# Retention in a two-layer trunk: rotation tables times R made once, one sum on GpSimd behind the swap, rotated tiles by turns of the pairs, y passes and stores later

## The chip, the cores and the metric

The kernel runs on one core of a Trainium2 chip. The core has five engines with an instruction queue each: TensorE (PE in the profile; PEld is its weight loads), VectorE (DVE), ScalarE (ACT), GpSimd (POOL) and SyncE (SP). SyncE here does little but issue DMA transfers, in order. An engine works through its queue in order, so an instruction that waits holds up all that stand behind it. The metric is the time of the program on the device in microseconds (us), median of several runs.

## The reference

A trunk of two layers on x of 1024 frames by 1024 channels, in float32. Layer 0 projects the normalised input to six parts and feeds two branches; the part that the change touches is retention, with rotary positions on q and k:

```python
def rope(x, positions):
    ...
    x1, x2 = x[..., :half], x[..., half:]
    return jnp.concatenate([x1 * cos - x2 * sin, x1 * sin + x2 * cos], axis=-1)

def retention(q, k, v):
    q = rope(q.astype(f32), positions) * (RET_DK ** -0.5)
    k = rope(k.astype(f32), positions)
    ...
    scores = jnp.einsum('bnihd,bnjhd->bnhij', qc, kc) * intra
    intra_out = jnp.einsum('bnhij,bnjhe->bnihe', scores, vc)
    kv = jnp.einsum('bnjhd,jh,bnjhe->bnhde', kc, k_dec, vc)
    ...
    _, s_prev = lax.scan(state_step, zeros, kv)
    cross = jnp.einsum('bnihd,ih,bnhde->bnihe', qc, q_dec, s_prev)
    out = normalised per head of (intra_out + cross)

def s5_mixer(u, ...):
    y = scan over chunks of a diagonal complex state space
    y = jax.nn.gelu(y)
    y = y * jax.nn.sigmoid(y @ glu_w + glu_b)
```

There are 8 heads of 64 (k, q) and 128 (v) channels, and 16 chunks of 64 frames. Each branch is multiplied by its SiLU gate, both go through one output projection, and layer 1 is a convolution module. R below is the reciprocal root mean square of each frame in layer 0: the projections run on x as it is, and their results are multiplied by R.

## The kernel before

**Arithmetic.** A float32 product is made of three matmuls with tiles split into a high and a low part (`mm3`: high by high, high by low, low by high). So every weight load `wf_…` is followed by a cast `wh_…` on ScalarE (L252) and a subtraction `wl_…` on GpSimd or VectorE (L253), and a projection of 128 channels by 512 frames (a half) is 24 matmuls into one PSUM bank, `mm_…`. The projections use a pool of 3 banks, most other products a pool of 5.

**Stages of layer 0.** The S5 scan and the gate projections fill the first 308 us. Then come the value products (`mm_v`, L1360) with sums of parts of x (`xt1` to `xt4`, a Strassen-like scheme), then four pairs of heads. A pair is projected (k, then q) while TensorE works through the heads of the pair before. The GLU of the S5 branch (`mm_glu`) begins before pair 3 ends, with a scheme of the same kind: it needs sums of weights (`gs`, written to DRAM as `ws_d`) and of y (`yn`, written as `yn_d` and, as differences, `t_d`).

**A pair (`ret_proj`, `ret_heads`).** VectorE writes `kraw` or `qraw` = bank times R, a half at a time (L1242). Rotation needs each 32-row block's partner, so four DMAs on SyncE write `kswp`/`qswp`, the tile with its blocks swapped (L1251, 128 KB each). GpSimd multiplies raw by the cosine table (L1255, into `krot`/`qrot`) and the swapped tile by the sine table (L1257), and VectorE adds them (L1258): 4 GpSimd and 2 VectorE instructions a tensor. The tables, `ropek`, are 1 MB, loaded at the start of the stage. Then TensorE transposes krot (`ktp`, L1372), VectorE scales it (`kt`, L1374), and TensorE makes `kv` (L1391), from which VectorE steps the state `S` (L1399, L1401), and the scores `sp` from qrot and krot (L1408); VectorE masks them (`sc`, L1414), and TensorE makes the output `ro` (L1435, L1440). It is normalised on VectorE and ScalarE (`bn`, `rs`, `off`, `on`; L1449 to L1457), transposed (`rt`), multiplied by the gate (`grl`, L1468) and stored (`yr_d`, L1471).

**The y passes (`y_pass`, L1125 to L1160).** The S5 output lies in DRAM in 8 blocks. Pass k (0 to 3) takes blocks k and k+4: load (`yp`, L1134), gelu on ScalarE (L1144), store of `yn_d` (L1146), four 128x512 subtractions on VectorE (L1150 to L1153), and for each of the two a high part `th` on ScalarE (L1157), its store (L1158), a low part on VectorE (L1159) and its store (L1160). Passes 0 and 1 run among the value products, a step at a time; passes 2 and 3 behind pairs 0 and 1, all through one buffer, tag `yp`: the load of block k+4 waits for the gelu of block k, and the second high part for the store of the first.

**What sets the order.** The program is written in one sequence, and a scheduler sorts it into the queue of each engine. `issue_after` holds instructions behind another, and the table `ORDER` names pairs on an engine: in (engine, late, early) the instruction of the one tile comes behind that of the other. Tiles with the same tag share `bufs` buffers, so that a new one waits for the readers of the old. `self.late` collects stores that `flush` issues some stages later, on SyncE.

Of the kernel before, what the change touches and what calls it, by code (L numbers as in the profile page):

```python
# [11 lines left out]
F32 = mybir.dt.float32  # L12
# [3 lines left out]
ALU = mybir.AluOpType  # L16
# [3 lines left out]
P = 128  # L20
# [18 lines left out]

LANES = 2  # L40
ORDER = (
    ('PE', ('turn', 0), ('mm_u6_0', 23)),
# [7 lines left out]
    ('DVE', ('cv6_0', 23), ('h1l0_1', 0)),  # L50
    ('SP', ('yt2h0', 0), ('qswp_3', 3)),
    ('PE', ('mm_oc2_1_0', 2), ('mm_oc0_1_0', 6)),
    ('DVE', ('mm_gluy3', 1), ('mm_gluz0', 0)),
# [74 lines left out]
class Trunk:  # L128
# [995 lines left out]
    def y_pass(self, k, yp=None, tag="ynt"):  # L1124
# [24 lines left out]
        (b11, b12), (b21, b22) = ((y[:, :HALF], y[:, HALF:]) for y in yns)  # L1149
        v.tensor_tensor(b22, b22, b12, op=ALU.subtract)  # L1150
        v.tensor_tensor(b12, b12, b11, op=ALU.subtract)
        v.tensor_tensor(b11, b22, b11, op=ALU.add)
        v.tensor_tensor(b21, b11, b21, op=ALU.subtract)  # L1153
        yield
# [8 lines left out]
    def glu_sums(self, g):  # L1163
# [13 lines left out]
        for i in range(2):  # L1177
            nc.sync.dma_start(self.ws_d[i, m, :, :, c].rearrange("p j k n -> p j (k n)"), q[i])

    def retention(self, st):  # L1180
# [5 lines left out]
        self.rk = rq.tile([P, 2, T], F32, name="ropek")  # L1186
        nc.sync.dma_start(self.rk[:], A["rope_k"])
        self.g128 = rp.tile([P, 4], F32, name="g128")
        nc.sync.dma_start(self.g128[:], A["ret_g128"])
# [8 lines left out]
        V = self.ret_values(vw)  # L1198
        for n, steps in enumerate(((0,), (0,), (1,), (1,), (1,), ())):
            next(V)  # L1200
            with self.tc.issue_after(self.last_evac.ins) if n == 3 else nullcontext():
                for i in steps:
                    next(y[i])
# [24 lines left out]
    def ret_proj(self, pair):  # L1228
        nc, A, rp = self.nc, self.A, self.rp
        mask = rp.tile([P, 2, P], F32, name=f"retmask_{pair}", tag="retmask", bufs=2)  # L1230
        nc.sync.dma_start(mask[:], A["ret_mask"][:, 2 * pair:2 * pair + 2])
        kdec = self.kdec[:, 2 * pair:2 * pair + 2]
        raws, tabs = {}, {"k": self.rk, "q": self.rk}

        def project(nm):
            w = self.wnext(f"{nm}{pair}")
            raw = raws[nm] = self.rq.tile([P, T], F32, name=f"{nm}raw_{pair}", tag="raw", bufs=2)
            for h in range(2):
                c = slice(h * HALF, (h + 1) * HALF)
                ps = self.bank(f"mm_{nm}{pair}_{h}", aux=False)  # L1240
                self.gemm(ps[:], w, self.xs[h])
                self.last_raw = nc.vector.tensor_tensor(nat(raw[:, c]), un(ps[:]), nat(self.R[:, c]), op=ALU.mult)  # L1242
            return self.last_raw

        def turn(nm, behind=None):
            raw, tab = raws[nm], tabs[nm]
            swp = self.rq.tile([P, T], F32, name=f"{nm}swp_{pair}", tag="swp", bufs=2)
            o = rp.tile([P, T], F32, name=f"{nm}rot_{pair}", tag=f"{nm}rot", bufs=1)
            for b in range(4):
                s = b ^ 1  # L1250
                self.last_swap = nc.sync.dma_start(swp[32 * b:32 * b + 32, :], raw[32 * s:32 * s + 32, :])  # L1251
            cs = [slice(h * HALF, (h + 1) * HALF) for h in range(2)]

            for c in cs:
                nc.gpsimd.tensor_tensor(o[:, c], raw[:, c], tab[:, 0, c], op=ALU.mult)  # L1255
            for c in cs:
                self.last_turn = nc.gpsimd.tensor_tensor(swp[:, c], swp[:, c], tab[:, 1, c], op=ALU.mult)  # L1257
            return o, [lambda c=c: nc.vector.tensor_tensor(o[:, c], o[:, c], swp[:, c], op=ALU.add) for c in cs]  # L1258


        project("k")
        yield None
        krot, adds = turn("k")
        last = project("q")
        with self.tc.issue_after(last.ins):
            for add in adds:
                add()
        qrot, qadds = turn("q")
        if pair % 2 == 0:
            for add in qadds:  # L1270
                add()
            qadds = ()
        yield krot, qrot, qadds, mask, kdec

    def ret_values(self, vw):
# [8 lines left out]
        def sums(name, k0, h):  # L1284
            res = []
            for i in range(2):
                f = self.rq.tile([P, 2, HALF], F32, name=f"{name}f{i}", tag="raw", bufs=2)
                nc.sync.dma_start(f[:], self.tx_d[k0 + 2 * i:k0 + 2 * i + 2, :, cs(h)].rearrange("k p t -> p k t"))
                for k in range(2):
                    a, b = (self.op_tile(vw, "t", f"{name}{q}{2 * i + k}") for q in "hl")  # L1290
                    nc.scalar.copy(a[:], f[:, k])
                    nc.gpsimd.tensor_tensor(b[:], f[:, k], a[:].bitcast(F32), op=ALU.subtract)
                    res.append((a, b))
# [769 lines left out]
def _shape_constants():  # L2063
# [5 lines left out]
    cos, sin = np.cos(ang), np.sin(ang)  # L2069
    rope = np.stack([np.concatenate([cos, cos] * 2, 0), np.concatenate([-sin, sin] * 2, 0)], 1)  # L2070
    c["rope_k"] = rope.astype(f)
# [73 lines left out]
```

## Time and profile before

| | |
|---|---|
| median of 3 runs | 1147.41 us (1146.99 to 1149.24) |
| profiled execution, and its span | 1148.62 us, 1146.5 us |
| granted TensorE clock, mean | 0.991 |
| value products | about 333 to 411 us |
| four pairs of heads | about 411 to 562 us |
| GLU of the S5 branch | about 532 to 633 us |

The page gives the busy time of each engine and its costliest groups. In a row of a timeline the first two numbers are start and length in us, then the engine, the line, the operation, out<-in, the number of instructions, and in brackets the idle time ahead and what ended it. Only an idle TensorE costs time directly: it is the engine that is nearly always busy.

### The profile page before, as it was taken

How to read it: one execution, taken by the hardware profiler on the slowest of the kernel's cores; microseconds unless marked ns; L12 is line 12 of the kernel's file. 1: busy time of each engine (PE TensorE's matmuls, PEld its weight loads, DVE VectorE, ACT ScalarE, POOL GpSimd, SP SyncE). 2: the span in 40 equal slices, each digit the busy share in tenths (PEclk: the TensorE clock that was granted, in tenths of full speed). 3: DMA queues.
4: the chain of work that ended last, by engine and by line, in shares of the span. 5: the costliest groups of instructions: out<-in, count | busy, mean ns of one | idle time of the engine just before them, and what ended most of it. 6: DMA issues, size and time to landing. Idle time of an engine off the chain costs nothing.

```text
span 1146.5 us, 16992 instructions
## 1 busy us (share of the span) xinstructions
PE 1109.6 (97%) x6014; PEld 965.9 (84%) x6014; DVE 831.2 (73%) x1444; ACT 543.8 (47%) x835; POOL 662.9 (58%) x463
## 2 busy tenths in 40 slices
PE   9999999999997998898899999999999999999997
PEld 8888888888885887777788888888888888888886
DVE  7877767777426564869558731499999989999744
ACT  7323334443224724425536523555544667446773
POOL 3059957878425425756377011389643468788863
PEclk9999999999998999999999999999999999999999
DMA  8445667776988656696998998566678665356964
GB/s 314 118 138 162 205 222 250 245 260 247 322 239 280 222 200 202 225 344 227 373 381 309 331 335 283 192 239 203 223 256 296 236 210 192 120 176 229 332 239 172
DMA packets 136117, 279.48 MB, mean 244 GB/s; under 512 B 21088, under 2 KB 50016, under 8 KB 135904
## 3 DMA queue, kind: packets, MB, share of 16 engines
q1 hardware_dynamic: 129744, 257.16, 66.8%
q10 hardware_dynamic: 6288, 21.24, 4.7%
q8 instruction: 47, 0.77, 0.3%
q14 instruction: 38, 0.31, 0.1%
HBM read 191.65 MB, written 82.51 MB: 239 GB/s over the span
## 4 chain that ended last, share of the span: by engine, by line
PE 76%; DMA 10%; DVE 5%; ACT 4%; issue 2%; POOL 2%; SPq 1%; POOLq 0%; ACTq 0%; DVEq 0%
PE mm_g L274 6%; PE mm_g L275 6%; PE mm_g L276 6%; PE mm_wo L274 5%; PE mm_wo L275 5%; PE mm_wo L276 5%; PE mm_v L1360 3%; PE mm_b L275 2%; PE mm_b L276 2%; PE mm_a L276 2%; PE mm_a L275 2%; PE mm_a L274 2%; PE mm_b L274 2%; PE mm_u L276 2%; PE mm_u L275 2%
## 5 line engine op out<-in xcount | busy, mean ns | idle before, releaser
L1762 DVE SCALAR_TENSOR_TENSOR cv<-u,convw,cv 128x512 f32<-128x512 f32 x390 | 267.7, 748 | 6.0 <-ACT cv L1729 3.9
L1723 POOL TENSOR_TENSOR tp<-tp,tp 128x512 f32<-128x512 f32 x64 | 82.4, 1288 | 33.1 <-ACT tp L1722 32.2
L274 PE MATMUL mm_g<-xh,wh_g 128*128 128x512 f32 x256 | 97.7, 382 | 0.0
L275 PE MATMUL mm_g<-xl,wh_g 128*128 128x512 f32 x256 | 97.0, 379 | 0.0
L276 PE MATMUL mm_g<-xh,wl_g 128*128 128x512 f32 x256 | 95.9, 379 | 0.0
L541 POOL TENSOR_TENSOR s1q<-s1q,s1q 128x512 f32<-128x512 f32 x12 | 16.7, 1391 | 81.0 <-ACT s1q L536 81.0
L1722 ACT ACTIVATE tp<-u,convw 128x512 f32<-128x512 f32 x64 | 45.3, 718 | 32.1 <-POOL tp L1723 31.3
L276 PEld LDWEIGHTS mm_g<-xh,wl_g 128*128 128x128 f32 x256 | 48.4, 189 | 6.9
L274 PEld LDWEIGHTS mm_g<-xh,wh_g 128*128 128x128 f32 x256 | 48.4, 189 | 6.9 <-issue 0.2
L275 PEld LDWEIGHTS mm_g<-xl,wh_g 128*128 128x128 f32 x256 | 48.4, 189 | 6.6
L275 PE MATMUL mm_oc<-zl,wh_woc 128*128 128x512 f32 (+1 forms) x144 | 51.4, 357 | 0.2 <-DVE zl L1477 0.2
L274 PE MATMUL mm_oc<-zh,wh_woc 128*128 128x512 f32 (+1 forms) x144 | 51.0, 363 | 0.0
L276 PE MATMUL mm_oc<-zh,wl_woc 128*128 128x512 f32 (+1 forms) x144 | 50.8, 356 | 0.0
L253 POOL TENSOR_TENSOR wl_glu<-wf_glu,wh_glu 128x1024 fp32r<-128x1024 f32 x14 | 33.8, 2422 | 27.1 <-DMA wf_glu<-ws_d 12.3
L274 PE MATMUL mm_wo<-ysh,wh_wos 128*128 128x512 f32 x128 | 48.9, 382 | 0.0
L274 PE MATMUL mm_g<-h1h,wh_cg 128*128 128x512 f32 x128 | 48.9, 382 | 0.0
L275 PE MATMUL mm_wo<-ysl,wh_wos 128*128 128x512 f32 x128 | 48.5, 379 | 0.0
L274 PE MATMUL mm_a<-h1h,wh_ca 128*128 128x512 f32 x128 | 48.5, 379 | 0.0
L276 PE MATMUL mm_wo<-ysh,wl_wos 128*128 128x512 f32 x128 | 48.5, 379 | 0.0
L276 PE MATMUL mm_b<-h1h,wl_cb 128*128 128x512 f32 x128 | 48.5, 379 | 0.0
L276 PE MATMUL mm_g<-h1h,wl_cg 128*128 128x512 f32 x128 | 48.5, 379 | 0.0
L275 PE MATMUL mm_a<-h1l,wh_ca 128*128 128x512 f32 x128 | 48.5, 379 | 0.0
(647 smaller groups left out, 3550.8 us busy)
## 6 DMA issues: line engine op xcount, KB each, us to landing
wf_g<-w_ab SPq DMA_DIRECT2D x16, 512.0 KB
wf_wos<-w_out SPq DMA_DIRECT2D x16, 512.0 KB
wf_wor<-w_out SPq DMA_DIRECT2D x16, 512.0 KB
wf_cb<-w_c SPq DMA_DIRECT2D x16, 512.0 KB
wf_ca<-w_c SPq DMA_DIRECT2D x16, 512.0 KB
wf_woc<-w_out_c SPq DMA_DIRECT2D x16, 512.0 KB
wf_cg<-w_c SPq DMA_DIRECT2D x11, 512.0 KB
x<-xT SPq DMA_DIRECT2D x8, 512.0 KB
```

Source lines behind the costliest of these rows:

```text
L253: self.low_made = lo[i].tensor_tensor(wl[:].rearrange(fl)[:, c], wf[:, c], h.bitcast(F32), op=ALU.subtract)
L274: nc.tensor.matmul(ps, wh[:, kb, :], xh, start=start, stop=False, **more)
L275: nc.tensor.matmul(ps, wh[:, kb, :], xl, start=False, stop=False, **more)
L276: self.last_mm = nc.tensor.matmul(ps, wl[:, kb, :], xh, start=False, stop=stop, **more)
L541: nc.gpsimd.tensor_tensor(a, a, sq[:], op=ALU.add)
L1360: nc.tensor.matmul(us[b][:], l[:, o], r, start=fresh and k == n == 0, stop=k == 3 and n == 2, **({} if fresh else {"skip_group_check": True}))
L1722: nc.scalar.mul(sk[:], u[:, k:k + HALF], cw[:, nb, k:k + 1])
L1723: gp.tensor_tensor(s0[:], s0[:], sk[:], op=ALU.add)
L1762: v.scalar_tensor_tensor(dst[:], *tap, accs_[i][:], op0=ALU.mult, op1=ALU.add)
```

## The change

- The tables are multiplied by R once: four 128x512 multiplications on GpSimd behind the load (L1217 of the changed kernel). From a bank VectorE then writes two products, raw (bank times the sine table) and the rotated tile (bank times the cosine table), L1275. The swap moves the product, so the signs of the sine table are turned round in the host's constants, and one addition a half on GpSimd (L1282) ends the rotation.
- raw and swapped tiles have one buffer each instead of two. krot and qrot of even pairs lie in one pool and those of odd pairs in another; the loads `xt…f` take the buffers of the odd ones instead of those of raw.
- Steps of y passes 0 and 1 stand two to four turns of the value products later. The four subtractions of passes 2 and 3 run on GpSimd. Stores of `ws_d` go to `self.late`.
- ORDER gains 23 rows. They put stores (`ws_d`, `yr_d`) and loads (`gs`, `grl`) of SyncE behind the swaps of pairs 1 to 3, the subtractions of passes 2 and 3 behind the q sums of pairs 1 and 2, casts of y behind others of ScalarE, and output products of pair 2 behind the q projection of pair 3.

```diff
+ADDS = {"k": lambda nc: nc.gpsimd, "q": lambda nc: nc.gpsimd}
 ORDER = (
...
+    ('SP', ('grl_6', 0), ('qswp_3', 3)),
+    ('Pool', ('yn_6', 0), ('qrot_1', 1)),
...
+    ('SP', ('ws_d', 6), ('qswp_3', 3)),
...
+    ('PE', ('ro0_4', 0), ('mm_q3_1', 23)),
+    ('Activation', ('th0_3', 0), ('on_5_1', 3)),
...
@@ y_pass
-        v.tensor_tensor(b22, b22, b12, op=ALU.subtract)
...
+        eng = nc.gpsimd if held else v
+        eng.tensor_tensor(b22, b22, b12, op=ALU.subtract)
...
@@ glu_sums
         for i in range(2):
-            nc.sync.dma_start(self.ws_d[i, m, :, :, c].rearrange("p j k n -> p j (k n)"), q[i])
+            self.late.append((1, lambda i=i: nc.sync.dma_start(self.ws_d[i, m, :, :, c].rearrange("p j k n -> p j (k n)"), q[i])))
@@ retention
         nc.sync.dma_start(self.rk[:], A["rope_k"])
+        for n in (1, 0):
+            for c in (slice(0, HALF), slice(HALF, T)):
+                nc.gpsimd.tensor_tensor(self.rk[:, n, c], self.rk[:, n, c], self.R[:, c], op=ALU.mult)
...
-        for n, steps in enumerate(((0,), (0,), (1,), (1,), (1,), ())):
+        for n, steps in enumerate(((), (), (0,), (0, 1), (1,), (1,))):
@@ ret_proj
+            raw = self.rq.tile([P, T], F32, name=f"{nm}raw_{pair}", tag="raw", bufs=1)
+            swp = self.rq.tile([P, T], F32, name=f"{nm}swp_{pair}", tag="swp", bufs=1)
+            o = (rp if pair % 2 else self.rq).tile([P, T], F32, name=f"{nm}rot_{pair}", tag=f"{nm}rot{pair % 2}", bufs=1)
...
-                self.last_raw = nc.vector.tensor_tensor(nat(raw[:, c]), un(ps[:]), nat(self.R[:, c]), op=ALU.mult)
+                for n, dst in ((1, raw), (0, o)):
+                    last = nc.vector.tensor_tensor(nat(dst[:, c]), un(ps[:]), nat(self.rk[:, n, c]), op=ALU.mult)
...
-                nc.gpsimd.tensor_tensor(o[:, c], raw[:, c], tab[:, 0, c], op=ALU.mult)
-            for c in cs:
-                self.last_turn = nc.gpsimd.tensor_tensor(swp[:, c], swp[:, c], tab[:, 1, c], op=ALU.mult)
-            return o, [lambda c=c: nc.vector.tensor_tensor(o[:, c], o[:, c], swp[:, c], op=ALU.add) for c in cs]
+                self.last_turn = eng(nc).tensor_tensor(o[:, c], o[:, c], swp[:, c], op=ALU.add)
@@ ret_values
-                f = self.rq.tile([P, 2, HALF], F32, name=f"{name}f{i}", tag="raw", bufs=2)
+                f = self.rp.tile([P, 2, HALF], F32, name=f"{name}f{i}", tag=f"{'kq'[i]}rot1", bufs=1)
```

How the queues change is shown at three places. The number behind a name's last underscore is the instance of a tile; "x2" is two like instructions. On VectorE, between the q projection of pair 1 and its first state step, there stood before:

```order
L1242 TENSOR_TENSOR qraw_1_4316<-mm_q1_1_4343,R0_356 128x512
L1258 TENSOR_TENSOR krot_1_4301<-krot_1_4301,kswp_1_4300 128x512 x2
L1150 TENSOR_TENSOR yn_6_4410<-yn_6_4410,yn_2_4404 128x512
L1151 TENSOR_TENSOR yn_2_4404<-yn_2_4404 128x512
L1152 TENSOR_TENSOR yn_2_4404<-yn_6_4410,yn_2_4404 128x512
L1242 TENSOR_TENSOR kraw_2_4643<-mm_k2_0_4644,R0_356 128x512
L1153 TENSOR_TENSOR yn_6_4410<-yn_2_4404,yn_6_4410 128x512
L1374 TENSOR_TENSOR kt_1_4426<-ktp0_1_4427,kdec_3344 128x512
L1374 TENSOR_TENSOR kt_1_4426<-ktp1_1_4433,kdec_3344 128x512
L1159 TENSOR_TENSOR yn_2_4404<-yn_2_4404,th0_2_4418 128x1024
L1258 TENSOR_TENSOR qrot_1_4372<-qrot_1_4372,qswp_1_4371 128x512 x2
L1242 TENSOR_TENSOR kraw_2_4643<-mm_k2_1_4670,R0_356 128x512
```

and now stands:

```order
L1275 TENSOR_TENSOR qraw_1_4316<-mm_q1_1_4346,ropek_3340 128x512
L1275 TENSOR_TENSOR qrot_1_4318<-mm_q1_1_4346,ropek_3340 128x512
L1388 TENSOR_TENSOR kt_1_4420<-ktp0_1_4421,kdec_3348 128x512
L1388 TENSOR_TENSOR kt_1_4420<-ktp1_1_4427,kdec_3348 128x512
L1275 TENSOR_TENSOR kraw_2_4639<-mm_k2_0_4642,ropek_3340 128x512
L1275 TENSOR_TENSOR krot_2_4641<-mm_k2_0_4642,ropek_3340 128x512
L1413 COPY S_1_4433<-kv0_1_4434 128x128
L1415 SCALAR_TENSOR_TENSOR S_1_4433<-S_1_4433,g128_3346,kv0_1_4434 128x128 x3
```

The four subtractions of y pass 2 (L1150 to L1153) and the additions of the rotation (L1258) are gone from here, the low part of y (L1159) stands further back, and each bank has two evacuations.

On GpSimd, at the same place of the program, there stood (behind the cosine products of q):

```order
L253 TENSOR_TENSOR wl_vm_4639<-wf_vm_4637,wh_vm_4638 128x1024
L1257 TENSOR_TENSOR qswp_1_4371<-qswp_1_4371,ropek_3340 128x512 x2
L1173 TENSOR_TENSOR gs1_0_4382<-gs1_0_4382 128x512
L1174 TENSOR_TENSOR gs1_0_4382<-gs0_0_4381,gs1_0_4382 128x512
L1175 TENSOR_TENSOR gs0_0_4381<-gs1_0_4382,gs0_0_4381 128x512
```

and now:

```order
L279 TENSOR_TENSOR wl_vm_4631<-wf_vm_4629,wh_vm_4630 128x1024
L1282 TENSOR_TENSOR qrot_1_4318<-qrot_1_4318,qswp_1_4317 128x512 x2
L1200 TENSOR_TENSOR gs1_0_4380<-gs1_0_4380 128x512
L1177 TENSOR_TENSOR yn_6_4404<-yn_6_4404,yn_2_4398 128x512
L1201 TENSOR_TENSOR gs1_0_4380<-gs0_0_4379,gs1_0_4380 128x512
L1178 TENSOR_TENSOR yn_2_4398<-yn_2_4398 128x512
L1202 TENSOR_TENSOR gs0_0_4379<-gs1_0_4380,gs0_0_4379 128x512
L1179 TENSOR_TENSOR yn_2_4398<-yn_6_4404,yn_2_4398 128x512
L1203 TENSOR_TENSOR gs0_0_4379<-gs0_0_4379 128x512
L1180 TENSOR_TENSOR yn_6_4404<-yn_2_4398,yn_6_4404 128x512
```

The k sum of pair 1 now stands ahead of the weights wl_vm; the subtractions of y pass 2 stand among the sums of GLU weights, by turns.

On TensorE, where pair 3 begins (`mm_glu11` is a product of the GLU, `rt` the transposes of the heads of pair 2), there stood:

```order
L274 MATMUL mm_glu11_5526<-y11h3_5491,wh_glu0_5104 128x512
L1372 MATMUL ktp0_3_5246<-ident_69,krot_3_5163 128x128 x4
L1372 MATMUL ktp1_3_5252<-ident_69,krot_3_5163 128x128 x4
L275 MATMUL mm_glu11_5526<-y11l3_5492,wh_glu0_5104 128x512
L276 MATMUL mm_glu11_5526<-y11h3_5491,wl_glu0_5105 128x512
L1391 MATMUL kv0_3_5265<-v_00_3507,kt_3_5245 64x128 x8
L1391 MATMUL kv1_3_5278<-v_01_3508,kt_3_5245 64x128 x6
L1408 MATMUL sp00_3_5290<-qrot_3_5236,krot_3_5163 128x128
L1408 MATMUL sp01_3_5291<-qrot_3_5236,krot_3_5163 128x128
```

and now:

```order
L302 MATMUL mm_glu11_5514<-y11h3_5479,wl_glu0_5093 128x512
L1479 MATMUL rt0_5_5063<-ident_69,on_5_0_5000 128x128 x4
L1479 MATMUL rt0_4_5069<-ident_69,on_4_0_4980 128x128 x4
L1479 MATMUL rt1_5_5075<-ident_69,on_5_1_5058 128x128 x4
L1479 MATMUL rt1_4_5081<-ident_69,on_4_1_5038 128x128 x4
L1386 MATMUL ktp0_3_5236<-ident_69,krot_3_5103 128x128 x4
L1386 MATMUL ktp1_3_5242<-ident_69,krot_3_5103 128x128 x4
L1405 MATMUL kv0_3_5253<-v_00_3507,kt_3_5235 64x128 x8
L1405 MATMUL kv1_3_5266<-v_01_3508,kt_3_5235 64x128 x6
L1422 MATMUL sp00_3_5278<-qrot_3_5174,krot_3_5103 128x128
L1422 MATMUL sp01_3_5279<-qrot_3_5174,krot_3_5103 128x128
```

The GLU products between ktp, kv and sp of pair 3 now stand ahead of them, and so do the transposes of pair 2. Before, 12 more GLU products stood between the first row of sp10_3 and the first of sp11_3; they no longer do.

64 lines of the change are left out of this document (35 added, 29 removed).

## The prediction

> **What bounds the kernel now.** I read the page first, for the engine that carries the span, then the waits of that engine, then its busy time by stage.
>
> ```profile
> span 1146.5 us, 16992 instructions
> PE 1109.6 (97%) x6014; PEld 965.9 (84%) x6014; DVE 831.2 (73%) x1444; ACT 543.8 (47%) x835; POOL 662.9 (58%) x463
> ```
>
> TensorE is busy for 1109.6 of 1146.5 us, so at most 36.9 us of the span can be had by taking its waits away, plus whatever a higher clock gives. The profiled execution took 1148.62 us, 2.1 more than its span, and lies 1.2 above the median of the runs, 1147.41. All terms below are taken from 1148.62, and 1.2 is subtracted at the end. The waits of TensorE between 308 and 562 us (engine, line, the one waited for; total, times, longest) say where the idle time is:
>
> ```profile
> PE kv L1391 <- DVE kt L1374: 5.9, 3, 4.4
> PE sp L1408 <- DVE qrot L1258: 5.9, 3, 5.1
> PE mm_v L1360 <- ACT v L1310: 5.7, 2, 2.9
> PE sp L1408 <- DVE S L1401: 2.9, 2, 1.6
> PE mm_v L1360 <- DVE wl_vc L253: 1.8, 1, 1.8
> PE ktp L1372 <- DVE krot L1258: 1.8, 2, 1.1
> PE mm_v L1360 <- DVE wl_vj L253: 1.7, 1, 1.7
> ```
>
> These seven rows add to 25.7 us: 70% of all TensorE idle time stands in this stretch, which is also where the change works. No row is long; each is an in-order engine that had something else in front. The windows (us, busy time and count of PE, PEld, DVE, ACT, POOL; granted clock, DMA share, GB/s) split it by stage:
>
> ```profile
> 344.00:410.00 66.00, 56.64 (x242) 47.85 (x243) 38.78 (x35) 35.62 (x50) 32.06 (x21) 0.92 0.80 269
> ...
> 449.00:472.00 23.00, 15.86 (x115) 13.15 (x114) 17.47 (x22) 4.32 (x4) 16.08 (x8) 0.93 0.77 256
> ...
> 530.00:562.00 32.00, 25.37 (x190) 21.39 (x189) 25.58 (x51) 8.84 (x20) 11.60 (x8) 0.95 0.88 301
> 562.00:626.00 64.00, 62.99 (x298) 54.45 (x297) 42.47 (x72) 37.46 (x61) 45.66 (x27) 1.00 0.97 353
> ```
>
> TensorE idles 9.4 us in the value products, 7.1 in pair 1, 6.6 in pair 3, and in the GLU stage behind them 1.0, where the DMA engines are 0.97 busy: there is no room for more bytes there. No engine is full in the stages with waits, so they are latency and order, not throughput.
>
> **The change part by part.** Durations first, from the tile views (shortest, median, longest ns of one):
>
> ```profile
> L1242 DVE TENSOR_TENSOR kraw<-mm_k,R x8: 668/684/693, 317.3 to 525.9; 128x512 f32<-128x512 f32 x8
> L1255 POOL TENSOR_TENSOR krot<-kraw,ropek x8: 1269/1278/2264, 325.7 to 526.7; 128x512 f32<-128x512 f32 x8
> L1257 POOL TENSOR_TENSOR qswp<-qswp,ropek x8: 1260/1351/2244, 349.9 to 546.3; 128x512 f32<-128x512 f32 x8
> L1258 DVE TENSOR_TENSOR qrot<-qrot,qswp x8: 676/1741/1765, 354.6 to 548.9; 128x512 f32<-128x512 f32 x8
> L1150 DVE TENSOR_TENSOR yn<-yn,yn x4: 692/692/1767, 340.1 to 509.6; 128x512 f32<-128x512 f32 x4
> ```
>
> *Work.* VectorE gains 16 evacuations from PSUM (16 x 0.68 = 10.9 us) and loses 16 additions (16 x 0.68 to 16 x 1.74, 10.9 to 27.8) and 8 y subtractions (8 x 0.69 = 5.5). So it is relieved by 5 to 22 us. GpSimd loses 32 multiplications (32 x 1.28 = 41) and gains 4 on the tables, 16 sums and 8 subtractions (28 x 1.28 = 36). Neither engine bounds a stage, so this sum is worth nothing by itself; what counts is what stands ahead of an operation that TensorE waits for.
>
> GpSimd's elementwise row is 1.28 us where VectorE's is 0.68. The Trainium skill ("GPSIMD Engine Reference", on elementwise work) speaks against such a move: two-input arithmetic costs about twice as much there; the rows agree, and by it alone the 8 q sums on the way to sp would take 8 x 0.6 = 4.8 us longer and the time would be 1141 instead of 1136, an estimate. The L1258 row is why I charge nothing for it: the same addition has a median of 1.74 us on VectorE, and its 0.68 is only met where GpSimd stands still.
>
> *Value products, 308 to 410.* The gaps are 1.1 (ktp), 5.7 (V copies), 1.8 and 1.7 (low weight halves). What stands ahead:
>
> ```profile
> 344.65 1.04 ACT L1157 CAST th<-yn 128x1024 fp32r<-128x1024 f32 x1
> ...
> 347.07 1.54 ACT L1310 COPY v<-mm_v 128x512 f32<-128x512 f32 x3
> 358.55 0.62 ACT L1291 CAST xt2h<-xt2f 128x512 fp32r<-128x512 f32 x1 [9.94 <-DMA xt2f<-tx_d]
> 359.07 0.58 ACT L1310 COPY v<-mm_v 128x512 f32<-128x512 f32 x1
> ```
> ```profile
> 345.73 2.28 DVE L1159 TENSOR_TENSOR yn<-yn,th 128x1024 fp32r<-128x1024 f32 x1
> 347.94 2.28 DVE L253 TENSOR_TENSOR wl_vc<-wf_vc,wh_vc 128x1024 fp32r<-128x1024 f32 x1
> ```
>
> Casts of y stand ahead of the V copies on ScalarE, and low parts of y ahead of wl_vc on VectorE. With the y steps two to three turns later both are gone, and the xt2f load is no longer tied to the raw buffers. Of 10.3 us I leave 1.0 for the copy behind xt2h (0 to 2.2) and take 9.3. Clock: 0.08 x 66 = 5.3 us at full effect; part of it lies in the gaps, so I take 1.3. Against it stand three new costs. The first evacuations now need the tables times R:
>
> ```profile
> 325.75 2.50 POOL L1255 TENSOR_TENSOR krot<-kraw,ropek 128x512 f32<-128x512 f32 x2 [8.82 <-DMA ropek<-rope_k]
> ```
>
> The table lands at 325.7; four multiplications of 1.25 to 1.3 end at 330.9. mm_k0_0 was evacuated at 317; now its bank is held 12 us longer. The three banks of that pool then hold up the q0 projection, though 12 value products stand ahead of it (12 x 0.22 = 2.6) and other products too: 0 to 5, I take 1.5. Later y steps now fall on the xt4 and xt1 loads in SyncE's queue and on the ScalarE casts of wh_vk, with the DMA share already 0.80: from −1 to 7, I take 3.5, midway, for want of a nearer row. Net gain 9.3 + 1.3 − 1.5 − 3.5 = **5.6** (0 to 12).
>
> *Pair 1, 449 to 472.*
>
> ```profile
> 459.64 3.17 PE L1391 MATMUL kv<-v,kt 128*64 128x128 f32 x28 [4.37 <-DVE kt L1374]
> ```
> ```profile
> 457.22 0.68 DVE L1242 TENSOR_TENSOR kraw<-mm_k,R 128x512 f32<-128x512 f32 x1
> 457.82 1.16 DVE L1153 TENSOR_TENSOR yn<-yn,yn 128x512 f32<-128x512 f32 x1
> 458.91 1.27 DVE L1374 TENSOR_TENSOR kt<-ktp,kdec 128x512 f32<-128x512 f32 x2
> ```
>
> kt_1 stands behind the y subtractions and a kraw that waits for its projection; both leave VectorE's path (the order rows above). 7.1 us of idle time go, and the kv products fall back from 3.17 to the 1.75 that the same 28 take in pair 2:
>
> ```profile
> 504.42 1.75 PE L1391 MATMUL kv<-v,kt 128*64 128x128 f32 x28 [0.86 <-DVE kt L1374]
> ```
>
> That is 1.4 more. The Trainium skill ("TensorE: Matmul & The Clock Gate", the HAM clock gate) has TensorE drop to half rate after an idle window of some 3.4 us; 3.17 against 1.75 behind a gap of 4.37 agrees. Late next: the q sum, behind four swaps and wl_vm on GpSimd (1 to 2.5), and the y subtractions, which share GpSimd with the glu sums (8 rows at 1.3 to 1.7 ahead of th0_2 and hence of th1_2 and the normalised tiles behind them on ScalarE: 0.5 to 2.5). I leave 3.2. Gain 7.1 + 1.4 − 3.2 = **5.3** (2 to 8.5).
>
> *Pair 2.* The 0.86 above and 1.3 before sp are behind VectorE; the q3 projection now stands between. Gain **2.1** (0 to 2.1).
>
> *Pair 3, 530 to 562.*
>
> ```profile
> 548.29 2.27 PE L1408 MATMUL sp<-qrot,krot 64*128 64x128 f32 x18 [5.10 <-DVE qrot L1258]
> ```
> ```profile
> 545.12 2.48 POOL L1257 TENSOR_TENSOR qswp<-qswp,ropek 128x512 f32<-128x512 f32 x2 [6.07 <-DMA qswp<-qraw]
> ```
> ```profile
> 517.91 1.05 ACT L1157 CAST th<-yn 128x1024 fp32r<-128x1024 f32 x1 [4.84 <-DMA t_d<-th]
> ```
>
> The q swaps were split by stores in SyncE's queue and landed at 545.1; those stores now follow them. So 6.6 us go, and 0.9 of clock. But GLU products no longer fill the places among ktp, kv and sp, and the tail of the y pass (th0_3, its store, th1_3: 4.84 us between) now falls here: rt of head 5 waits for its last normalised tile (1.6), kt_3 behind one y subtraction of 1.2 to 2.8 (1.6), S_3 behind another (2.7), the next GLU weights without filler (1.2): 7.1 lost. Gain **0.4** (−3 to 5).
>
> *GLU, 562 to 626.* Six stores of 0.5 MB move from before 562 to behind it: 3 MB at the 353 GB/s of the window are 8.5 us of a stage that has 3% to spare. It is hidden as long as weights run ahead; TensorE idled only 1.0 there, so they did. I charge 2 (0 to 8.5).
>
> **Sum:** 5.6 + 5.3 + 2.1 + 0.4 − 2.0 = 11.4; 1148.6 − 11.4 = 1137.2, less 1.2 is **1136 us**.
>
> **The rivals.**
> 1. *Half of it comes back.* The y subtractions on GpSimd cost pair 1 all of 5 us and the value stage's loads 7: 11.4 − 1.8 − 3.5 = 6, so about 1141. For it: the DMA share of 0.80 to 0.88. Against: GpSimd is idle for 7 of 23 us in pair 1.
> 2. *All gaps close.* Every wait of the table (25.7), and 1.4 + 0.9 + 1.3 of clock, less 1.5 for the tables and 3.2 in pair 1: 24.6, so 1123. For it: none of the stages has a full engine. Against: pair 3 has lost its filler. By the clock gate's rule the windows' whole missing clock (5.3 + 1.6 + 1.6 us) would be had back as well, an estimate of 5 us more.
> 3. *Nothing.* The change doesn't relieve TensorE: the waits go over to the swaps' landing, which takes as long as before (the 6.07 of GpSimd), and the delayed stores fill the GLU stage with 8.5: 11.4 − 8.5 − 3 = 0, 1147.
> 4. *Slower.* The y chain runs through one buffer: high part, its store, second high part, its store, next load, gelu, load, gelu, store, and only then the y21f load, with the q swaps of pair 3 behind it in SyncE's queue.
>
> ```profile
> 502.71 2.11 ACT L1144 ACTIVATE yn<-yp 128x512 f32<-128x512 f32 x2 [5.80 <-DMA yp<-y_d]
> ```
> ```profile
> 530.84 1.75 SPq L1499 DMA_DIRECT2D y21f<-yn_d  x4
> ```
>
> ```profile
> 333.89 0.33 ACTq L1146 DMA_DIRECT2D yn_d<-yn  x1
> ```
> ```profile
> 340.05 0.69 DVE L1150 TENSOR_TENSOR yn<-yn,yn 128x512 f32<-128x512 f32 x1 [11.74 <-DMA yn_d<-yn]
> ```
>
> The last gelu ended at 504.8 and its rows were loaded at 530.8; with a store of 6 us (333.9 to 340.0 in pass 0) that leaves some 19 us of cover. Subtractions on GpSimd and the stores between use about 10 of it. Beyond the remaining 9 every microsecond shows ahead of sp of pair 3; from a further slip of 20 (9 of cover and the gain of 11.4) the kernel is slower than before. At 26 it takes 1153. The point of no gain is therefore a y21f load at about 551. Against it: that takes two more landings of 8 us (this gelu still waited 5.80 for its load) than I count.
>
> **How the numbers follow.** Forecast (1131 to 1140) 0.47; rival 1 0.22; rival 2 0.10; rival 3 0.09; rival 4 0.12. The range 1124 to 1147 leaves out rival 4 and half of rival 2. A measurement of this kernel can tell about 0.2%, 2.3 us, from no change: faster 0.79, same 0.09, slower 0.12.
>
> **What would show it.** In the profile of the changed kernel: no wait of mm_v on V copies or on wl_vc; kv of pair 1 without a gap over 1 us and at 1.75; sp of pair 3 waiting less than 2 us for the q sum but ktp, kv and S there together for 4 to 6; the GLU window with a DMA share of 0.97 or more and under 3 us idle. The prediction is wrong if the q0 projection waits over 5 us for a bank, if the value stage still idles over 7 us, or if y21f is issued after 545.

## The result and the profile after

The changed kernel took 1135.96 us (median of 4 runs, 1135.55 to 1137.54) beside 1147.59 for the kernel before: a ratio of 0.9899, interval 0.9882 to 0.9916. The forecast was 1136, from a sum of four gains and one loss. The sum came out; two of its terms did not, and their errors, of opposite sign, nearly cancel.

The page, and TensorE's waits (engine, line, the one waited for; total, times, longest) from 300 to 560 us:

```profile
span 1133.7 us, 16979 instructions
...
PE 1105.6 (98%) x6014; PEld 963.9 (85%) x6014; DVE 812.3 (72%) x1436; ACT 543.2 (48%) x835; POOL 657.0 (58%) x459
```
```profile
PE sp L1422 <- DVE sc L1428: 4.7, 1, 4.7
PE mm_glu L302 <- POOL wl_glu L279: 4.1, 3, 3.2
PE sp L1422 <- POOL qrot L1282: 2.6, 3, 1.2
PE rt L1479 <- ACT on L1471: 2.6, 2, 1.4
PE kv L1405 <- DVE kt L1388: 1.8, 1, 1.8
PE mm_v L1374 <- DVE v L1342: 1.0, 1, 1.0
PE mm_q L300 <- DVE krot L1275: 0.2, 1, 0.2
```

The span fell by 12.8 us. TensorE's busy time fell by 4.0 of these, for the same 6014 matmuls, mostly by the clock (0.991 before, 0.994 after, as means of the span). Its idle time fell by 8.8. The waits of the value products (V copies, wl_vc, wl_vj) are gone and a late V scaling of 1.0 is left; kv and sp of pair 1 no longer wait for VectorE's y work. In their place stand waits at pair 3 and in the GLU.

Time by stage needs places that have the same work ahead of them in both kernels. Five matmuls serve, on the timeline of TensorE (start, length in us); here in the kernel after:

```profile
311.54 0.46 PE L300 MATMUL mm_k<-xh,wh_k 128*128 128x512 f32 x1
...
402.97 1.20 PE L1405 MATMUL kv<-v,kt 128*64 128x128 f32 x18
...
464.95 0.38 PE L1360 MATMUL mm_w<-wh_vm,xh 128*128 128x512 f32 x1
...
519.32 0.88 PE L1405 MATMUL kv<-v,kt 128*64 128x128 f32 x12 [1.80 <-DVE kt L1388]
...
613.36 0.38 PE L300 MATMUL mm_wo<-ysh,wh_wos 128*128 128x512 f32 x1
```

In the kernel before they start at 311.80, 416.88, 485.67, 541.45 and 626.33. Between each two stand the same matmuls, apart from the order within. The forecast's terms are set against the same stretches (of pair 3, its losses ahead of kv fall into the third stretch, the rest into the last):

| stretch | before | after | change | forecast |
|---|---|---|---|---|
| first mm_k to kv of pair 0 (value products) | 105.1 | 91.4 | −13.7 | −5.6 |
| kv of pair 0 to mm_w (pair 1) | 68.8 | 62.0 | −6.8 | −5.3 |
| mm_w to kv of pair 3 | 55.8 | 54.4 | −1.4 | −0.3 |
| kv of pair 3 to mm_wo (rest of pair 3, GLU) | 84.9 | 94.0 | +9.2 | −0.1 |

So 21.9 us were won ahead of pair 3 and 9.2 lost behind it. Of the 9.2, 6.5 are idle time of TensorE, and the rest is longer matmuls at a lower clock (the last stretch as a window, before and after: length, busy time of PE, PEld, DVE, ACT, POOL; granted clock, DMA share, GB/s):

```profile
541.45:626.33 84.88, 78.77 (x436) 68.43 (x437) 56.92 (x110) 41.35 (x70) 50.58 (x29) 0.98 0.98 355
```
```profile
519.32:613.36 94.04, 81.44 (x436) 69.29 (x437) 63.88 (x107) 44.36 (x74) 56.60 (x31) 0.95 0.95 343
```

The two longest gaps after stand at sp and at mm_glu. The kernel before had one of 5.10 at sp as well, for the q sum, so the gap at sp alone is no loss yet. On the timelines of VectorE, GpSimd, TensorE and SyncE of the kernel after (in brackets the idle time ahead and what ended it):

```profile
519.78 6.35 DVE L1491 TENSOR_TENSOR y21l<-y21f,y21h 128x512 fp32r<-128x512 f32 x4
526.05 2.28 DVE L1186 TENSOR_TENSOR yn<-yn,th 128x1024 fp32r<-128x1024 f32 x1
528.25 0.28 DVE L1413 COPY S<-kv 128x128 f32<-128x128 f32 x1
528.45 1.27 DVE L1428 TENSOR_TENSOR sc<-sp,retmask 128x512 f32<-128x512 f32 x2
```
```profile
529.18 1.86 PE L1422 MATMUL sp<-qrot,krot 64*128 64x128 f32 x13 [4.74 <-DVE sc L1428]
...
554.46 0.48 PE L302 MATMUL mm_glu<-y21h,wl_glu 128*128 128x512 f32 x1 [3.22 <-POOL wl_glu L279]
```
```profile
517.14 2.05 POOL L1200 TENSOR_TENSOR gs<-gs 128x512 f32<-128x512 f32 x1 [10.31 <-DMA yt2l<-t_d]
...
525.66 1.59 POOL L1203 TENSOR_TENSOR gs<-gs 128x512 f32<-128x512 f32 x1
```
```profile
505.31 0.61 SPq L1197 DMA_DIRECT2D gs<-w_glu  x1
...
520.59 7.29 SPq L1205 DMA_DIRECT2D ws_d<-gs  x2
...
533.25 0.44 SPq L276 DMA_DIRECT2D wf_glu<-w_glu  x1
```

SyncE needs 7.29 us for two issues that elsewhere take 0.6 each: it stands before the stores of the last weight sums, which GpSimd finishes at 527.3. The loads of the next GLU weights are queued behind.

### The profile page after: what moved, and what is told of

The parts are those of the page before. It is cut to its first block, busy times and chain, and to the rows that moved or that the text cites. A ratio compares the mean times of both kernels' runs of the same rounds, so it can differ in the third digit from the quotient of the medians.

```text
span 1133.7 us, 16979 instructions
## 1 busy us (share of the span) xinstructions
PE 1105.6 (98%) x6014; PEld 963.9 (85%) x6014; DVE 812.3 (72%) x1436; ACT 543.2 (48%) x835; POOL 657.0 (58%) x459
## 4 chain that ended last, share of the span: by engine, by line
PE 85%; DMA 5%; DVE 3%; ACT 2%; POOL 2%; issue 2%; SPq 0%; POOLq 0%; DVEq 0%; ACTq 0%
PE mm_g L300 7%; PE mm_g L302 7%; PE mm_g L301 7%; PE mm_v L1374 5%; PE mm_wo L302 5%; PE mm_wo L300 5%; PE mm_wo L301 5%; PE mm_b L301 2%; PE mm_b L302 2%; PE mm_a L301 2%; PE mm_b L300 2%; PE mm_a L302 2%; PE mm_a L300 2%; PE mm_u L301 2%; PE mm_u L300 2%; PE mm_u L302 2%
## 5 line engine op out<-in xcount | busy, mean ns | idle before, releaser
L302 PE MATMUL mm_a<-h1h,wl_ca 128*128 128x512 f32 x128 | 48.6, 379 | 0.0
L301 PE MATMUL mm_g<-h1l,wh_cg 128*128 128x512 f32 x128 | 48.6, 379 | 0.0
```

The lines of the kernel that those rows point to most:

```text
L301: nc.tensor.matmul(ps, wh[:, kb, :], xl, start=False, stop=False, **more)
L302: self.last_mm = nc.tensor.matmul(ps, wl[:, kb, :], xh, start=False, stop=stop, **more)
```

## The experiments

Each kernel ran beside the kernel before on the same chip, and times of different chips are compared by their ratio to it; "stretch" is one of the four above, read in the profile of the run.

**1. Undo the y subtractions on GpSimd** (and the two ORDER rows that pin them there).

```diff
-        eng = nc.gpsimd if held else v
+        eng = v
```

> The changed kernel with one part undone: the four subtractions of y passes 2 and 3 are on VectorE again (and the two ORDER rows for them on GpSimd go). In the profile of the changed kernel the stretch from the first kv of pair 0 to the first mm_w is 62.0 us against 68.8 before, with the same matmuls in it. If the subtractions ahead of kt_1 and S_1 on VectorE made the waits of pair 1, the stretch is 65 to 69 us and a gap of over 2 us stands ahead of kv or sp of pair 1 again. If it was the rotation's additions on VectorE, it stays at 61 to 63. For the total: if what comes later (from kv of pair 3 to the first mm_wo, 94.0 us against 84.9 before) is paced by queues on the core, the loss goes through, 1139 to 1142; if it is paced by the DMA transfers, the later stretch shrinks by as much and the total is 1135 to 1138.

1136.86 us, ratio 0.9907 (0.989 to 0.9925): not to be told from the changed kernel. The second stretch went to 69.2 (with eight transposes that stood in the third before), which is all of the gain in pair 1, but the last one fell from 94.0 to 88.0. TensorE shows the wait in pair 1:

```profile
450.26 1.83 PE L1420 MATMUL sp<-qrot,krot 64*128 64x128 f32 x13 [5.87 <-DVE S L1413]
```

and the one of 4.74 before sp of pair 3 is down to 1.15. The same four y21l and the same low part stand ahead of S and sc there, but they take 3.10 and 1.21 us instead of 6.35 and 2.28. TensorE comes to kv of pair 3 at 527.0, 7.6 us later than in the changed kernel, and the last sums of GLU weights on GpSimd end at 528.2, only 0.9 later; most of the y21l now run when GpSimd has finished. So what is won in pair 1 lets TensorE come to pair 3 before those sums are done: won once, paid once. The total is that of the second case. Whether transfers pace the later stretch is left to (8) to (10).

**2. to 4. What carries the value products?** The y steps put back, without their three ORDER rows (2), the steps with these rows alone in the kernel before (3), and the sums of x in the raw and swapped tiles' buffers again (4):

```diff
-        for n, steps in enumerate(((), (), (0,), (0, 1), (1,), (1,))):
+        for n, steps in enumerate(((0,), (0,), (1,), (1,), (1,), ())):
```
```diff
-                f = self.rp.tile([P, 2, HALF], F32, name=f"{name}f{i}", tag=f"{'kq'[i]}rot1", bufs=1)
+                f = self.rq.tile([P, 2, HALF], F32, name=f"{name}f{i}", tag=("raw", "swp")[i], bufs=1)
```

> The changed kernel with the steps of y passes 0 and 1 where they were before among the value products (and the three ORDER rows that pin them gone). The stretch from the first mm_k of pair 0 to the first kv is 91.4 us in the changed kernel and 105.1 before, with the same 419 rows on TensorE. If the y casts and low parts ahead of the V copies and the weights' low parts carry that gain, the stretch is 99 to 105 us; if it is the loads of the sums of x, which no longer wait for the raw buffers, it is 91 to 94. The total: 1143 to 1150 by the first if later stages pass the loss on, 1138 to 1141 if the later stretch is paced by DMA transfers and absorbs most of it, 1135 to 1138 by the second.

> The kernel before with nothing but the later steps of y passes 0 and 1 and their three ORDER rows. If these steps carry the value products' gain, the stretch from mm_k of pair 0 to kv falls from 105.1 to 92 to 96 us and the total to 1136 to 1141 (or to 1142 to 1146 if it is given back behind pair 3); if the buffers of the sums of x carry it, the stretch stays above 101 us.

> The changed kernel with the loads of the sums of x put into the raw and swapped tiles' buffers again, so that they wait for the rotation of pair 0. If the freed buffers carry the value products' gain, the stretch from mm_k of pair 0 to kv goes from 91.4 to 98 to 106 us; if the steps of the y passes do, it stays at 91 to 94 us. The total follows as in the run before: passed on in full, or absorbed behind pair 3.

| kernel | time | ratio to before | first stretch | last stretch |
|---|---|---|---|---|
| changed | 1135.96 | 0.9899 (0.9882 to 0.9916) | 91.4 | 94.0 |
| 2: changed, old steps | 1141.15 | 0.9954 (0.9937 to 0.997) | 99.3 | 93.6 |
| 3: before, new steps | 1141.71 | 0.9955 (0.994 to 0.9971) | 96.3 | 86.3 |
| 4: changed, x sums in raw buffers | 1142.46 | 0.9964 (0.995 to 0.9978) | 99.4 | 93.3 |

Neither theory alone holds: each part, taken out of the changed kernel, costs 8 us of the first stretch. Run 12, which has the new rotation with neither part (what else it leaves out acts later), completes the square. Its first stretch is 98.8; with the freed buffers alone it is 99.3 (2), with the new steps alone 99.4 (4), with both 91.4. So in the kernel with the new rotation one part by itself gains nothing, and the two together 7.4. In the kernel before, the steps alone give 8.8 (3). In (2) and (4) TensorE waits for the same instruction, the V copy on ScalarE that holds the PSUM banks. With the old steps (2), casts of y stand ahead of it:

```profile
345.58 1.04 ACT L1181 CAST th<-yn 128x1024 fp32r<-128x1024 f32 x1 [4.02 <-DVE yn L1176]
...
347.48 0.58 ACT L1321 COPY v<-mm_v 128x512 f32<-128x512 f32 x1
```

with the raw buffers (4), a cast that waits for a load:

```profile
349.85 0.62 ACT L1305 CAST xt2h<-xt2f 128x512 fp32r<-128x512 f32 x1 [7.70 <-DMA xt2f<-tx_d]
350.38 0.58 ACT L1324 COPY v<-mm_v 128x512 f32<-128x512 f32 x1
```

TensorE waits 4.00 us there in (2) and 3.22 in (4): with one obstacle left, the other's removal stays hidden. The freed buffers were not tried in the kernel before. In (2) and (4) TensorE comes to pair 3 seven us later and the last stretch is unchanged. But the last sums of GLU weights end six to seven us later as well (534.0 and 533.4 instead of 527.3), so these two runs do not tell what sets that stretch.

**5. The rotation's sums on VectorE** (`ADDS` with `nc.vector` for both; two ORDER rows go with it, as the expectation says).

> The changed kernel with the 16 sums behind the swaps on VectorE instead of GpSimd (0.68 us alone against 1.28). If the longer latency on GpSimd costs on the way to sp, the waits of sp for the q sum (2.6 us in all) fall below 1.5 us and the total falls to 1132 to 1134. If the additions on VectorE wait for the swaps ahead of kt and S, or take 1.7 us beside GpSimd, kt and S waits grow by 2 to 6 us in pairs 1 and 3 and the total is 1137 to 1143. Two ORDER rows that name the sums on GpSimd go, so the y subtractions are free to move ahead.

1142.36 us, ratio 0.9953 (0.9936 to 0.9969): the total of the second case, 6 us worse than the changed kernel. The waits stand elsewhere than it said: kt and S cost 1.1 us together, but TensorE waits 6.5 us for a normalised tile, whose statistics stand behind a q sum that waits 5.23 us for its swap; 3.6 for krot and 2.1 for qrot; and 4.8 at ro for sc, behind a low part of y. The additions wait on VectorE for the swaps, and two of them take 3.89 us beside GpSimd:

```profile
429.80 3.89 DVE L1280 TENSOR_TENSOR krot<-krot,kswp 128x512 f32<-128x512 f32 x2 [7.70 <-DMA kswp<-kraw]
```

The second and third stretch grow to 76.1 and 59.3, and the last falls to 83.3, of which more below (10).

**6. and 7. VectorE's queue and GpSimd's queue behind pair 3.** Two rows put the y21l and the low part of y behind state and scores; then one more puts a sum behind two weight halves:

```diff
+    ('DVE', ('y21l0', 0), ('sc1_3', 1)),
+    ('DVE', ('yn_7', 0), ('sc1_3', 1)),
```
```diff
+    ('Pool', ('yg0_0', 0), ('wl_glu4', 0)),
```

> The changed kernel with two more ORDER rows: on VectorE the four y21l and the last low part of y pass 3 come behind the state and the masked scores of pair 3. In the changed kernel the longest wait of pair 3 is 4.74 us of sp for sc, with 6.35 us of y21l and 2.28 of the low part (which waits for its high part) ahead of S_3 and sc on VectorE. If VectorE's queue makes that wait, it falls below 1 us, the stretch from kv of pair 3 to the first mm_wo goes from 94.0 to 88 to 91 us, and the total to 1131 to 1133. If the loss behind pair 3 is set by the transfers that the GLU waits for, or by the GLU products that no longer stand between sp rows, the wait comes back as one of mm_glu and the stretch stays at 93 to 95, 1135 to 1137.

> The run before with one more row: on GpSimd the sum yg0_0, which waits for a load, comes behind the low weight halves wl_glu3 and wl_glu4. In the changed kernel mm_glu waits 3.22 us for wl_glu while GpSimd stands before yg0_0. If the queue of GpSimd makes that wait, it goes, and the total is 2 to 3 us below the run before, 1128 to 1131; if the loads of the weights do (DMA share 1.04 in that stretch), it stays over 2 us and the total is that of the run before.

1135.74 and 1135.79 us, ratios 0.9897 (0.9881 to 0.9913) and 0.9899 (0.9882 to 0.9917): nothing. The wait for sc is gone, as the first theory has it, and waits of mm_glu take its place, as the second has it. TensorE and SyncE in (6):

```profile
533.14 0.48 PE L302 MATMUL mm_glu<-y11h,wh_glu 128*128 128x512 f32 x1 [2.48 <-ACT wh_glu L280]
...
535.57 0.80 PE L304 MATMUL mm_glu<-y11h,wl_glu 128*128 128x512 f32 x1 [1.72 <-POOL wl_glu L281]
...
556.31 0.80 PE L304 MATMUL mm_glu<-y21h,wl_glu 128*128 128x512 f32 x1 [5.11 <-POOL wl_glu L281]
```
```profile
538.66 0.69 SPq L1189 DMA_DIRECT2D t_d<-yn  x1
540.43 0.33 SPq L278 DMA_DIRECT2D wf_glu<-w_glu  x1
```

The weights of the GLU are the next limit. But the two rows make it worse by themselves: the low part that now comes later is stored later, and on SyncE the next weights stand behind that store. They are issued at 540.4 in (6) and 540.7 in (7), against 533.2 in the changed kernel. So these runs show that this order gains nothing; they do not show that the gap of 4.74 is worth nothing.

**8. Store the weight sums at once.** The six ORDER rows for `ws_d` go, and

```diff
-            self.late.append((1, lambda i=i: nc.sync.dma_start(self.ws_d[i, m, :, :, c].rearrange("p j k n -> p j (k n)"), q[i])))
+            nc.sync.dma_start(self.ws_d[i, m, :, :, c].rearrange("p j k n -> p j (k n)"), q[i])
```

> The changed kernel with the stores of the GLU weight sums (ws_d, eight of 0.5 MB) issued as soon as they are made again, without their six ORDER rows. The prediction charged 2 us (0 to 8.5) for the stores moved into the GLU stage. If they cost that stage, the stretch from kv of pair 3 to mm_wo goes from 94.0 to 86 to 92 us; against it, the swaps of pairs 2 and 3 wait behind stores, and sp of pair 3 waits 2 to 4 us more for the q sum. If the stores are hidden, the stretch stays at 93 to 97 and the total at 1135 to 1139.

1126.11 us, ratio 0.9816 (0.9799 to 0.9832). The queues of TensorE, VectorE and ScalarE are those of the changed kernel row for row; only SyncE and GpSimd differ. The last stretch went from 94.0 to 84.2, which is the whole gain, and the first three stayed (91.7, 62.2, 54.4). The feared waits for the q sum did not come: 0.9 us in all. TensorE's waits from 300 to 640 us:

```profile
PE rt L1473 <- ACT on L1465: 2.9, 2, 1.7
PE sp L1416 <- DVE sc L1422: 1.9, 1, 1.9
PE kv L1399 <- DVE kt L1382: 1.8, 1, 1.8
PE mm_v L1368 <- DVE v L1336: 1.0, 1, 1.0
PE sp L1416 <- POOL qrot L1276: 0.9, 1, 0.9
```

The wait of sp for sc fell from 4.74 to 1.88 us though VectorE's queue is the same, because the rows ahead of S and sc have become shorter:

```profile
519.73 2.49 DVE L1485 TENSOR_TENSOR y21l<-y21f,y21h 128x512 fp32r<-128x512 f32 x4
522.13 1.22 DVE L1180 TENSOR_TENSOR yn<-yn,th 128x1024 fp32r<-128x1024 f32 x1
```

In the changed kernel they took 6.35 and 2.28, while GpSimd worked on the last sums until 527.3. Here GpSimd has nothing to do from 515.8 to 532.0.

SyncE, for the loads and stores of the last weight sums and the next weights:

```profile
496.06 1.37 SPq L1191 DMA_DIRECT2D gs<-w_glu  x2
...
505.63 0.59 SPq L1199 DMA_DIRECT2D ws_d<-gs  x1
...
508.59 0.60 SPq L1199 DMA_DIRECT2D ws_d<-gs  x1
...
521.99 1.42 SPq L270 DMA_DIRECT2D wf_glu<-w_glu  x1
```

The sums are loaded at 496 instead of 505 to 507 and done at 508 instead of 527; these stores no longer hold up SyncE, and the next weights' load is issued at 522.0 instead of 533.2.

**9. and 10. The bytes or the chain?** The last group's stores alone late, the four ORDER rows of the other groups gone (9); and, in the changed kernel, the same two stores put behind the load wf_glu4 (10):

```diff
-            self.late.append((1, lambda i=i: nc.sync.dma_start(self.ws_d[i, m, :, :, c].rearrange("p j k n -> p j (k n)"), q[i])))
+            st = lambda i=i: nc.sync.dma_start(self.ws_d[i, m, :, :, c].rearrange("p j k n -> p j (k n)"), q[i])
+            self.late.append((1, st)) if g == 3 else st()
```
```diff
+    ('SP', ('ws_d', 6), ('wf_glu4', 0)),
+    ('SP', ('ws_d', 7), ('wf_glu4', 0)),
```

> With the weight sums stored at once the kernel took 1126.1 us instead of 1136.0: the stretch from kv of pair 3 to the first mm_wo fell from 94.0 to 84.2. Two theories. A, a chain through the buffers: each group of weight sums uses the two buffers of the group before, so late stores of group 2 make the loads and sums of group 3 late (505.3 and 517 to 527 us instead of 496 and 503 to 508), and SyncE stands 7.29 us before the stores of group 3 with the loads of the GLU weights behind. B, the bytes: 0.5 MB stores in the GLU stage take the transfers' time from its loads. Here only the last group's two stores stay late (behind the q swaps of pair 3), the other groups' go at once. By A the block goes, since the last sums are ready by 508 to 510: stretch 84 to 86, total 1125 to 1128. By B a part of the loss stays, about 2 of 6 stores: stretch 87 to 90, total 1128 to 1132.

> The changed kernel with the last group's two stores of weight sums put further back still, behind the load wf_glu4 on SyncE, so that nothing that loads the next GLU weights stands behind their wait. By A (SyncE stands before these stores for 7.29 us with wf_glu3 and wf_glu4 behind them) the waits of mm_glu for wh_glu and wl_glu near 554 go and the total falls to 1127 to 1132. By B (bytes in the GLU stage) nothing is won, 1135 to 1140, since the same bytes now fall still later.

(9) took 1127.73 us, ratio 0.983 (0.9811 to 0.985), last stretch 83.2: the total that theory A gave, with a stretch a little below its 84 to 86. Two stores stay behind the q swaps, and they cost nothing that can be told from (8), because the sums are ready:

```profile
510.31 1.27 SPq L1201 DMA_DIRECT2D ws_d<-gs  x2
```

What counted was that the stores of the groups before come early, since the last group is loaded into their buffers. As a test of B this run is weak, since its two stores go out only 2 to 5 us behind those of (8). B fails on the trace of the changed kernel, where all eight stores are issued by 527.9:

```profile
L1205 SPq DMA_DIRECT2D ws_d<-gs x8: 592/614/1357, 443.2 to 527.3; - x8
```

The stage from 562 in the kernel before is the last 64 us ahead of mm_wo. In the changed kernel these begin at 549, 21 us behind the last of the stores: no store has moved into the stage.

(10) took 1133.97 us, ratio 0.9881 (0.9863 to 0.99), which overlaps the changed kernel's and lies between the ranges of the two cases; last stretch 92.0. SyncE no longer stands before these stores, and the next weights are issued 8 us earlier:

```profile
524.97 0.38 SPq L278 DMA_DIRECT2D wf_glu<-w_glu  x1
```
```profile
568.64 0.80 PE L302 MATMUL mm_glu<-yt3h,wh_glu 128*128 128x512 f32 x1 [3.25 <-ACT wh_glu L280]
```

But the last sums are nearly as late as before (525.0), the y21l beside them take 6.22 us, sp still waits 4.02, and mm_glu waits 3.25 for weights. So the block on SyncE is a small part: some 2 us by the ratios, hardly clear of noise, of the 9.8 that (8) gains. What goes with the loss in all of these kernels is the end of the last sums on GpSimd, counted from the first kv of pair 3 on TensorE:

| kernel | last sums done | last stretch |
|---|---|---|
| changed, 2, 4, 6, 7, 10 | 6.1 to 7.9 us behind kv | 92.0 to 94.5 |
| 1 | 1.2 us behind | 88.0 |
| before, 3, 5, 8, 9, 11 | 7.8 to 17.3 us ahead | 83.2 to 86.7 |

The row of (5) tells most: it stores the sums as late as the changed kernel does, but TensorE comes to pair 3 19 us later, and the loss is gone. (12) is left out, since twelve GLU matmuls of its last stretch stand behind mm_wo. How the loss is shared between VectorE's longer rows beside GpSimd and the weights that come later was not tried apart.

**11. State first, with early stores.** The two rows of (6) in the kernel of (8).

> The kernel of 1126.1 us (weight sums stored at once) with the two rows that put the state and scores of pair 3 ahead of y21l and the low part on VectorE. With stores late these two rows only turned a wait of sp into waits of mm_glu. If the loads of the GLU weights set the pace there in that case alone, the remaining waits of sp and ro in pair 3 (1.9 and 0.5 us) now go and the total is 1123 to 1125; if the loads still set it, they come back as mm_glu and the total is 1126 to 1128.

1129.28 us, ratio 0.9841 (0.9823 to 0.9859): no gain, and by its ratio slightly worse than (8) (the intervals overlap), as neither case foresaw. The wait for sc went, but SyncE stands in the way, as in (6): the store of the low part that moved back is ahead of the weights' load, now issued at 530.8 instead of 522.0.

```profile
530.22 0.38 SPq L1183 DMA_DIRECT2D t_d<-yn  x1
530.85 0.33 SPq L272 DMA_DIRECT2D wf_glu<-w_glu  x1
```

**12. The rotation alone.** Tables, two products, one sum and tiles by turns; everything else as before, without the ORDER rows of the change (there are 25 of them, not 23 as written above).

> Of the change only the rotation itself: tables times R made once, two products out of PSUM, one sum on GpSimd, tiles by turns of the pairs. The y steps, the y subtractions on VectorE, the stores of weight sums and the buffers of the sums of x are as they were (these use the raw and swapped tiles' buffers), and the 23 ORDER rows are gone. If the rotation is worth something by itself, it is in pair 1, where the additions on VectorE go: stretch from kv of pair 0 to mm_w 62 to 66 us against 68.8, total 1139 to 1144. If its worth lies in the room it makes for the other parts, the total is 1145 to 1150.

1145.87 us, ratio 0.9984 (0.9971 to 0.9997): the second case. It relieves VectorE and GpSimd and gains some 3 us at most, and not in pair 1, whose stretch is 68.0. The waits move; the two longest stand before kv of pair 2 and before ktp of pair 3:

```profile
PE kv L1380 <- DVE kt L1363: 6.4, 1, 6.4
PE ktp L1361 <- POOL krot L1257: 3.9, 2, 3.3
```

The first stretch is 98.8 even so (105.1 before), though this kernel has neither the new steps nor the freed buffers, and the third is 65.9 (55.8 before). So 6.3 of the value products' 13.7 us come with the rotation itself; which of its edits carries them was not tried. The third stretch loses more than that, by the two waits shown, and the last is 75.9, with the twelve matmuls fewer.

The fastest version found is (8): the change without the late stores of the weight sums, 1.8% below the kernel before.

## Why the prediction was right, and where it was not

**What bounds.** Right: all of the gain is TensorE's waits and clock between 308 and 626 us, and the order of the queues decided it. The rotation, which names the change, is worth little alone (12). That the sums on GpSimd are charged with nothing, for all that one takes 1.28 us, was right: the kernel with them on VectorE is 6 us slower (5). The rule of the Trainium skill ("GPSIMD Engine Reference", on elementwise work) holds for one instruction, 1.28 against 0.68 us; here the queue decided against it.

**Value products: the term was mis-sized, 5.6 against 13.7.** The working had 9.3 of idle time go; 9.1 went. The three corrections were wrong. The tables' multiplications were charged 1.5 and cost 0.2 (the mm_q row above); the cover of 12 value products, which the working names, was enough. Later y steps were charged 3.5 "for want of a nearer row" and cost nothing visible: that midpoint of an unknown was simply too pessimistic. The clock was given 1.3; the rest of the stretch, 13.7 − 9.1 = 4.6, is matmuls that take less time, by the clock:

```profile
344.00:403.00 59.00, 58.03 (x272) 50.23 (x270) 35.41 (x39) 32.49 (x43) 27.80 (x17) 1.00 0.77 258
```

The granted clock (third number from the end) is 1.00 there, against 0.92 in the value products before. The 5.3 us "at full effect" were nearly right. The estimate of rival 2, which had the whole missing clock back, does better here than my cut to a quarter: a gap costs itself and the slow matmuls behind it. The Trainium skill ("TensorE: Matmul & The Clock Gate", the HAM clock gate) names an idle window of about 3.4 us for the fall to half rate. The gaps of the value products before were 2.9 us at most, and the clock fell all the same; so this trace shows the loss behind shorter gaps than the page names.

**Pair 1: right, 5.3 against 6.8.** kt no longer waits, kv runs at the fast rate (1.75 us for 28), the q sum costs 0.90 and rt waits 1.44 for a normalised tile, as listed. What the forecast missed is the price elsewhere: in run 1, with the subtractions on VectorE again, pair 1 loses 7.2 us and the last stretch gains 6.0.

**Up to kv of pair 3: right.** The gaps of pair 2 are gone; rt waits 1.16 and kt 1.80, against 1.6 each.

**Behind kv of pair 3: a step failed, −0.1 against +9.2.** "It is hidden as long as weights run ahead; TensorE idled only 1.0 there, so they did. I charge 2" looked at bytes alone, and its premise, "Six stores of 0.5 MB move from before 562 to behind it", did not come about: the last store is issued by 527.9. What the late stores do is hold the buffers of the next sums, so a late store is a late load, a late sum and late weights: the last sums end at 527.3 instead of 508.3, and stores issued at once give 9.8 us back (8). The term for S_3 named the right place (2.7 forecast, 4.74 measured) with a cause that was only half of it: the rows of y ahead of S_3 and sc stand there in (8) as well, but sp waits 1.88, since GpSimd no longer works beside them. The bound "0 to 8.5" for the stores nearly held the loss, by a mechanism that was not in it.

**The total was right because +8.1 and −9.3 cancel**; pair 1 and the third stretch add the other 2.6 us. So the mechanism was right up to pair 3, and that the total came out at 1136 is luck. Of the signs named for the profile, the waits of V copies and wl_vc (gone), kv of pair 1, the q sum of pair 3 (1.7 us) and y21f (issued by 505) came; ktp, kv and S of pair 3 waited 6.5 instead of 4 to 6, and the GLU idled 5.9 us instead of under 3. That last sign, written down beforehand, is what pointed at the failed step.

The rival "slower", through the single y buffer, did not occur: y21f was issued from 500.4. Rival 1's price was half there (the gain of the subtractions is paid back, though behind pair 3 and not in pair 1), rival 2's sign too (the first three stretches gave 21.9 of its 24.6), and run 8 with 1126 us is close to what rival 2 took for all gaps closed.

## What to carry to other kernels

A store that is put later holds its buffer; ask which load waits for that buffer and who waits for what is made from it, before counting the bytes. Before a row is moved to close a gap, ask who waits for what that row makes: in (6) and (11) the row that moved back was stored later, and the next loads stood behind its store. Where two parts of a change clear the same wait, try them in all four combinations; here each alone gains nothing beside the new rotation, and both 7.4 us. Where a correction is a midpoint between ends far apart, keep the sum without it beside the forecast, or two such corrections will hide each other's errors in a total that looks right.

## What the runs showed of the hardware

Two obstacles ahead of one instruction on an in-order queue do not add: with the new rotation the first stretch is 98.8 us with both, 99.3 or 99.4 with one and 91.4 with neither. VectorE's subtractions of two tiles take longer while GpSimd works: the four y21l took 6.35 us in the changed kernel, where GpSimd was on the last sums, and 2.49 in (8), where it stood still. And SyncE works through its queue in order like the other engines: two stores that waited for their data held it for 7.29 us, and the load behind them, issued at 533.2, went out at 525.0 once they were put behind it (10).
